# Two-layer encoder on one core: the residual stream kept with features along the partitions, weights stationary in the output projections and in the first MLP's way down

## The chip, the cores and the metric

One core of a Trainium2 chip runs the whole program. The metric is the device time of one launch in microseconds (us). The engines are named as in the profile: PE (matmul, with PEld for its weight loads), DVE (VectorE), ACT (ScalarE), POOL (GpSimd), SP (the DMA queue that loads the weights).

## What is computed

Two residual layers on 256 tokens of 1024 features in float32, each a mixer and an MLP, with RMSNorm before each and at the end:

```python
h = x
for layer in range(2):
    hn = rms_norm(h, norm_mix_g[layer])
    if layer == 0:   # 8 GQA heads and 8 dilated heads, one output projection
        mix = concatenate([o_a, o_b]) @ ab_w_out
    else:            # latent attention, 16 heads: hn @ c_w_down first, then up-projections
        mix = o_c @ c_w_out
    h = h + mix
    hn = rms_norm(h, norm_mlp_g[layer])
    h = h + square(relu(hn @ mlp_w1[layer])) @ mlp_w2[layer]     # 1024 -> 4096 -> 1024
return rms_norm(h, final_norm_g)
```

## The kernel before

Float32 products are made of three matmuls (`mm3`, lines 273 to 278): each operand is split into a high part that the PE reads in its one-pass float32 form and a low remainder, and high x high, high x low and low x high are summed in PSUM. Weights come in chunks of 2048 columns through SP; ACT casts the high half (`whi`, line 223), DVE subtracts for the low half (`wlo`, line 230), and eight buffers of each are held, so that a cast waits for the PE to give back the buffer of an earlier chunk.

A matmul has a stationary operand (128 x 128, loaded by PEld) and a moving one (up to 512 columns). Before the change the residual `xh` lies with tokens along the partitions (two tiles of 128 tokens x 1024 features). The two output projections (`out_first`, `out_second`, lines 545 to 574) and the way down of both MLPs (`down`, line 616) hold 128 tokens stationary and move 512 weight columns. A PSUM bank of 512 columns is one token tile `t` and one half `c` of the features. `residual` (line 508) adds a finished bank to `xh` on DVE. The next projection wants the features along the partitions, as `hT` (high and low, both views of `hTs`), so `turn` (line 516) transposes four 128 x 128 blocks on PE against `ident` (line 521), multiplies by the gain on DVE (line 525), casts on ACT (line 528) and subtracts on DVE (line 529). `Later` puts each turn a quarter of a chunk behind its bank. There are twelve turns: four after each output projection and four after the first MLP. All other projections (`rows` in the way up, lines 601 and 602; the latent down, line 1091; q up, line 1135) already hold the weights stationary.

Division by the root mean square is left to later: `mean_square` (line 350) takes squares of `xh` on ACT with a running sum per token, and the result is used per token in the residual of the MLP (`rs2`) or in `latent` (line 1099), where `rsqrt` on POOL (line 337) and a spread over the partitions (`row_scales`, line 364) follow on the matmuls with `ones` of lines 1102 and 1105. In the meantime PE works on the q up-projection.

In the first attention the order is written out by hand (`ORDER_AB`); elsewhere a scheduler places each engine's instructions by priority, and `tc.high_priority()` moves residual and turn ahead. Each engine runs its list in order. PSUM has four banks `mm`, two `s` and two `o`. `work` is a tile of 512 columns with five buffers.

Of the kernel before, what the change touches and what calls it, by code (L numbers as in the profile page):

```python
# [11 lines left out]
F32 = mybir.dt.float32  # L12
# [157 lines left out]
def encoder(ctx: ExitStack, tc: tile.TileContext, x, xg, wall, grow, const, onehot, relb, out):  # L170
# [116 lines left out]
    g = cp.tile([P, N_G], F32, name="g")  # L287
    xgt = ap.tile([P, N_G + KT * S], F32, name="xgt", tag="OT0")

# [20 lines left out]
    kc = cp.tile([P, N_K], F32, name="kc")  # L310
    xh = cp.tile([P, NT, D], F32, name="xh")
    for i in range(2):
# [29 lines left out]

    def squares(part, t, c):
        nc.scalar.activation(junk, xh[:, t, cols(c, 512)], AF.Square, accum_out=part[:, 2 * c + t:2 * c + t + 1])
# [4 lines left out]

    def mean_square(name):  # L350

        part, u = small(4), cp.tile([P, NT], F32, name=f"u{name}")
        for t in range(NT):
            for c in range(2):
                squares(part, t, c)
        mean_of(part, u)
        return u
# [149 lines left out]

    def residual(acc, t, c, scale=None):
        dst = xh[:, t, cols(c, 512)]
        with tc.high_priority():  # L510
            if scale is None:
                nc.vector.tensor_tensor(dst, acc, dst, op=OP.add)
            else:
                nc.vector.scalar_tensor_tensor(dst, acc, scale, dst, op0=OP.mult, op1=OP.add)

    def turn(c, t, gbase):

        with tc.high_priority():
            pt = t_bank()
            for q in range(4):  # L520
                nc.tensor.transpose(pt[:, cols(q)], xh[:, t, cols(4 * c + q)], ident)  # L521
            ks = slice(4 * c, 4 * c + 4)
            gt = work()
            gv, pv = (z.rearrange("p (k t) -> p k t", k=4) for z in (gt, pt))
            nc.vector.tensor_tensor(gv, pv, g[:, gbase + 4 * c:gbase + 4 * c + 4][:, :, None].to_broadcast([P, 4, P]),
                                    op=OP.mult)
            hi, lo = hT[0][:, ks, cols(t)], hT[1][:, ks, cols(t)]
            nc.scalar.copy(hi, gv)
            nc.vector.tensor_tensor(lo, gv, hi.bitcast(F32), op=OP.subtract)  # L529

    class Later:

        todo = None

        def put(self, *a):
            self.todo = a

        def flush(self):
            if self.todo is not None:
                turn(*self.todo)  # L540
                self.todo = None

    later = Later()
# [12 lines left out]

    def out_second(name, src, acc, gbase):
        last = None
        for c in range(2):
            i, w = take(name, 2 + c, 4)  # L560
            with ExitStack() as order:
                if last is not None:
                    order.enter_context(tc.issue_after(last.ins))
                for t in range(NT):
                    for k in range(4):
                        last = mm3(acc[c][t], tok(src, 4 + k, t), w(k), False, k == 3)
                        if k == 1:
                            quarter()
                            later.flush()
                    if t == 1:  # L570
                        done.add(i)
                    residual(acc[c][t], t, c)
                    later.put(c, t, gbase)
                    quarter()

    def mlp(l, final, store):
        h2, down_w = {}, {}
        acc = {}
        with tc.tile_pool(name=f"mlp{l}", bufs=3) as mp:
# [35 lines left out]

            def down(u, c, t):
                i, w = down_w[u]
                for k in range(2):
                    mm3(acc[c, t], tok(h2[u], k, t), w(k, cols(c, 512)), u + k == 0,
                        k == 1 and u == (14 if final and c == 1 else 15))  # L620

            first = [take(f"w1_{l}", 0, 8)]
            hb = [[s_bank() for _ in range(2)], [mm_bank() for _ in range(2)]]
            for ks in (range(4), range(4, 8)):
                for u in range(2):
                    if len(first) < 2 and u == 1:
                        first.append(take(f"w1_{l}", 1, 8))
                    for m in range(2):
# [5 lines left out]
                        quarter()  # L634
                        later.flush()
            rs2 = cp.tile([P, NT], F32, name=f"rs2{l}")
            nc.vector.reciprocal(rs2, mean_square(f"m{l}"))
            for c in range(2):
                for t in range(NT):
                    acc[c, t] = mm_bank()  # L640
            for u in range(2, 16):
                down_w[u - 2] = take(f"w2_{l}", u - 2, 2)
                for c in range(2):
                    for t in range(NT):
# [3 lines left out]
                        quarter()  # L648
                up(u)
            for u in (14, 15):  # L650
                down_w[u] = take(f"w2_{l}", u, 2)
            groups = [(c, t) for c in range(2) for t in range(NT)]
            if not final:
                for c, t in groups:
                    down(14, c, t)
                    quarter()
                    later.flush()
# [3 lines left out]
                    residual(acc[c, t], t, c, rs2[:, t:t + 1])  # L661
                    later.put(c, t, G_MIX + KT)
                    quarter()
# [390 lines left out]
    with tc.tile_pool(name="l1", bufs=1) as lp:  # L1054
# [29 lines left out]

        u1 = mean_square("c")
        for j in range(2):
            i, w = take("down", j, 4)
            for n, m in enumerate(order):
# [7 lines left out]
                quarter()  # L1096
                later.flush()

# [149 lines left out]
```

## Time and profile before

| | us |
|---|---|
| median of 3 runs (568.02 to 568.09) | 568.04 |
| the profiled execution | 567.76 |
| its span from first to last instruction | 566.0 |
| PE busy in the span | 555.5 |
| PEld / DVE / ACT / POOL busy | 461.6 / 399.1 / 328.5 / 33.5 |

Matmuls overlap in the pipe: one of 512 columns stays on record for 0.39 us while the next starts after 0.23. What a matmul costs a full PE is therefore the distance between starts, which is read from the timeline, and not its duration.

### The profile page before, as it was taken

Reading aid. Unit: us, or ns where it says so; the run is one execution under the profiler, and the core shown is the slowest. Engines: PE = TensorE matmul, PEld = TensorE weight load, DVE = VectorE, ACT = ScalarE, POOL = GpSimd, SP = SyncE. Lnnn points to the kernel's source line nnn. Section 1 sums busy time; section 2 is a strip of 40 time slices with the busy share of each in tenths; the row PEclk is TensorE's granted clock in tenths of the full one; section 3 lists DMA queues with packets and bytes.
Section 4 is the critical chain, followed back from the end, with each engine's and each line's share of the span. In section 5 each row is a group of like instructions: output and inputs, shape, how many; then the busy total and the mean of one; then the engine's idle time right before and its main releaser. Section 6 shows DMA issues by size and latency. Waiting matters only on the chain.

```text
span 566.0 us, 8115 instructions
## 1 busy us (share of the span) xinstructions
PE 555.5 (98%) x3044; PEld 461.6 (82%) x3044; DVE 399.1 (71%) x717; ACT 328.5 (58%) x612; POOL 33.5 (6%) x58
## 2 busy tenths in 40 slices
PE   8999999999999999999999999999999999999994
PEld 4899777888888888888889876678888888888884
DVE  4999978986675666566687987588667566656635
ACT  5879878755444454545464797655544445454513
POOL 3430000000000000000012000000000000000002
PEclk9999999999999999999999999999999999999999
DMA  8847344765555454646426222255555545554101
GB/s 287 356 157 240 125 150 155 259 212 193 174 198 203 170 203 173 218 156 218 167 107 247 75 76 75 75 186 174 198 173 200 201 170 204 172 219 153 71 1 74
DMA packets 16663, 97.16 MB, mean 172 GB/s; under 512 B 1858, under 2 KB 3650, under 8 KB 5872
## 3 DMA queue, kind: packets, MB, share of 16 engines
q1 hardware_dynamic: 15040, 94.38, 46.1%
q0 software_dynamic: 864, 1.20, 1.0%
q10 hardware_dynamic: 720, 1.07, 0.6%
q8 instruction: 24, 0.39, 0.3%
q14 instruction: 15, 0.12, 0.1%
HBM read 95.05 MB, written 1.06 MB: 170 GB/s over the span
## 4 chain that ended last, share of the span: by engine, by line
PE 89%; DMA 3%; ACT 3%; DVE 2%; POOL 1%; issue 1%; SPq 0%; POOLq 0%; DVEq 0%; ACTq 0%
PE s L601 20%; PE mm L276 15%; PE mm L278 15%; PE mm L277 15%; PE s L602 10%; PE s L1205 2%; DMA xh<-in_x 2%; PE o L408 2%; PE o L480 1%; PE o L469 1%; PE o L419 1%; DMA raw<-in_wall 1%; PE o L521 1%; PE mm L601 1%; ACT whi L223 1%
## 5 line engine op out<-in xcount | busy, mean ns | idle before, releaser
L230 DVE TENSOR_TENSOR wlo<-raw,whi 128x1024 fp32r<-128x1024 f32 (+1 forms) x182 | 208.8, 1163 | 96.1 <-ACT whi L223 95.6
L223 ACT CAST whi<-raw 128x1024 fp32r<-128x1024 f32 (+1 forms) x181 | 177.9, 1005 | 83.5 <-PE mm L278 39.1
L601 PE MATMUL s<-hTs,whi 128*128 128x512 f32 x480 | 168.5, 393 | 0.1
L602 PE MATMUL s<-hTs,wlo 128*128 128x256 f32 x480 | 134.3, 280 | 0.0
L601 PEld LDWEIGHTS s<-hTs,whi 128*128 128x128 f32 x480 | 90.2, 188 | 20.4 <-DVE hTs L529 0.4
L276 PE MATMUL mm<-whi,h2h 128*128 128x512 f32 x252 | 99.5, 395 | 0.0
L277 PE MATMUL mm<-wlo,h2h 128*128 128x512 f32 x252 | 99.5, 395 | 0.0
L278 PE MATMUL mm<-whi,h2l 128*128 128x512 f32 x252 | 99.0, 395 | 0.0
L602 PEld LDWEIGHTS s<-hTs,wlo 128*128 128x128 f32 x480 | 90.3, 188 | 1.3
L594 ACT CAST h2h<-work 128x256 fp32r<-128x256 f32 x64 | 25.6, 403 | 56.7 <-DVE work L593 56.7
L276 PEld LDWEIGHTS mm<-whi,h2h 128*128 128x128 f32 x252 | 47.5, 188 | 11.6 <-ACT h2h L594 0.9
L278 PEld LDWEIGHTS mm<-whi,h2l 128*128 128x128 f32 x252 | 47.4, 188 | 11.2 <-DVE h2l L595 0.3
L277 PEld LDWEIGHTS mm<-wlo,h2h 128*128 128x128 f32 x252 | 47.5, 188 | 9.5
L591 ACT COPY work<-s 128x256 f32<-128x256 f32 x60 | 22.2, 371 | 46.4 <-PE s L602 46.4
L592 DVE TENSOR_TENSOR work<-s,work 128x256 f32<-128x256 f32 x60 | 25.2, 420 | 17.1 <-ACT work L591 17.1
L595 DVE TENSOR_TENSOR h2l<-work,h2h 128x256 fp32r<-128x256 f32 x64 | 26.8, 421 | 14.6 <-ACT h2h L594 14.6
L593 DVE SCALAR_TENSOR_TENSOR work<-work 128x256 f32<-128x256 f32 x64 | 27.0, 424 | 2.0
L276 PE MATMUL mm<-whi,hTs 128*128 128x256 f32 (+1 forms) x80 | 27.2, 340 | 0.5 <-ACT hTs L992 0.5
L278 PE MATMUL mm<-whi,hTs 128*128 128x256 f32 (+1 forms) x80 | 26.7, 334 | 0.0
L276 PE MATMUL mm<-whi,OT 128*128 128x512 f32 x64 | 26.5, 414 | 0.0
L277 PE MATMUL mm<-wlo,hTs 128*128 128x256 f32 (+1 forms) x80 | 26.4, 330 | 0.0
L277 PE MATMUL mm<-wlo,OT 128*128 128x512 f32 x64 | 25.7, 401 | 0.0
(236 smaller groups left out, 759.4 us busy)
## 6 DMA issues: line engine op xcount, KB each, us to landing
raw<-in_wall SPq DMA_DIRECT2D x84, 1024.0 KB, 4.8
bias<-line_d SPq DMA_DIRECT2D x4, 384.0 KB, 6.0
raw<-in_wall SPq DMA_DIRECT2D x4, 256.0 KB, 5.8
raw<-in_wall SPq DMA_DIRECT2D x2, 512.0 KB, 7.0
xh<-in_x SPq DMA_DIRECT2D x1, 1024.0 KB, 11.1
xgt<-in_xg SPq DMA_DIRECT2D x2, 256.0 KB, 7.5
kc<-in_const SPq DMA_DIRECT2D x1, 512.0 KB, 8.3
kdB<-kdB POOLq DMA_DIRECT2D x4, 128.0 KB, 4.0
```

Source lines behind the costliest of these rows:

```text
L223: return cast(parts[i, q // 2][0][:, 512 * (q % 2):512 * (q % 2 + n)], raws[i][:, 512 * q:512 * (q + n)])
L230: nc.vector.tensor_tensor(lo[:, s], raws[i][:, 512 * q:512 * (q + n)], hi[:, s].bitcast(F32), op=OP.subtract)
L276: nc.tensor.matmul(out, ah, bh, start=first, stop=False)
L277: nc.tensor.matmul(out, ah, bl, start=False, stop=False)
L278: return nc.tensor.matmul(out, al, bh, start=False, stop=last)
L591: nc.scalar.copy(v[:, 0], bank[:, S:])
L592: nc.vector.tensor_tensor(v[:, 0], bank[:, :S], v[:, 0], op=OP.add)
L593: nc.vector.scalar_tensor_tensor(v[:, 1], v[:, 0], 0.0, v[:, 0], op0=OP.max, op1=OP.mult)
L594: nc.scalar.copy(hi, v[:, 1])
L595: nc.vector.tensor_tensor(lo, v[:, 1], hi.bitcast(F32), op=OP.subtract)
L601: nc.tensor.matmul(bank, wh, hTs[:, k].rearrange("p a t -> p (a t)"), start=k == 0, stop=False)
L602: nc.tensor.matmul(bank[:, S:], wl, hT[0][:, k], start=False, stop=k == 7)
```

## The change

The residual keeps the features along the partitions until the last MLP. The input tile `xgt`, which holds x in this layout, becomes a constant-pool tile and is the residual itself (`xr`); the token-major `xh` moves to the buffer `OT0` and serves the first layer's mean square and, again, the last MLP. The output projections and the first MLP's way down hold weight blocks of 128 x 128 stationary and move all 256 tokens, so each matmul of 512 columns becomes two of 256. `residual` adds a bank and makes `hT` at once from two feature tiles, on ACT (gain and cast) and DVE (gain and subtract); `turn` and `Later` are gone. Squares are summed by `Squares` on ACT and POOL; `spread` gives the mean to all partitions with two matmuls on `ones`, `by_token` gives it per token with four matmuls of one column. The last MLP still wants tokens along the partitions: `xgt` is transposed there, 16 blocks in four banks, and copied by ACT.

```diff
-    xgt = ap.tile([P, N_G + KT * S], F32, name="xgt", tag="OT0")
+    xgt = cp.tile([P, N_G + KT * S], F32, name="xgt")
+    xr = xgt[:, N_G:]
...
-    xh = cp.tile([P, NT, D], F32, name="xh")
+    xh = ap.tile([P, NT, D], F32, name="xh", tag="OT0")
...
+    def residual(bank, b, gbase, scale=None):
+        dst = xr[:, cols(b, 512)]
         with tc.high_priority():
+            if scale is not None:
+                v = work()
+                nc.vector.tensor_tensor(halves(v), halves(bank), scale[:, None, :].to_broadcast([P, 2, S]), op=OP.mult)
+                bank = v
+            nc.vector.tensor_tensor(dst, bank, dst, op=OP.add)
+            for k in (2 * b, 2 * b + 1):
+                gc = g[:, gbase + k:gbase + k + 1]
+                nc.scalar.activation(hT[0][:, k], xT(k), AF.Copy, scale=gc)
+                nc.vector.scalar_tensor_tensor(hT[1][:, k], xT(k), gc, hT[0][:, k].bitcast(F32),
+                                               op0=OP.mult, op1=OP.subtract)
...
+    class Squares:
+        def add(self, b):
+            if b == 0:
+                nc.scalar.activation(self.total, xr[:, cols(b, 512)], AF.Square)
+                return
+            sq = work()
+            nc.scalar.activation(sq, xr[:, cols(b, 512)], AF.Square)
+            nc.gpsimd.tensor_tensor(self.total, self.total, sq, op=OP.add)
+        def by_token(self):
+            pm, u = o_bank(), small(2, 12)
+            for t in range(NT):
+                for i in range(2):
+                    nc.tensor.matmul(pm[:, t:t + 1], self.total[:, S * i + P * t:S * i + P * t + P], ones[:, 0:1],
+                                     start=i == 0, stop=i == 1)
+            nc.vector.tensor_scalar(u, pm[:, :NT], 1.0 / D, EPS, op0=OP.mult, op1=OP.add)
+            return u
+        def spread(self):
+            pm, r = o_bank(), sp.tile([P, S], F32, name="rsb", tag="prob", bufs=3)
+            for i in range(2):
+                nc.tensor.matmul(pm[:, :S], ones, self.total[:, cols(i, S)], start=i == 0, stop=i == 1)
...
     def out_first(name, src, acc):
...
-                for t in range(NT):
-                    mm3(acc[c][t], tok(src, k, t), w(k), k == 0, False)
+                for m in range(4):
+                    mm3(acc[c][m // 2][:, cols(m % 2, S)], w(k, cols(m)), pair(src, ALL, k), k + m % 2 == 0, False)
...
             def down(u, c, t):
                 i, w = down_w[u]
                 for k in range(2):
-                    mm3(acc[c, t], tok(h2[u], k, t), w(k, cols(c, 512)), u + k == 0,
...
+                    else:
+                        for m in range(2):
+                            mm3(acc[c, t][:, cols(m, S)], w(k, cols(4 * c + 2 * t + m)), pair(h2[u], ALL, k),
+                                u + k + m == 0, u + k + m == 17)
...
+            if final:
+                xh = ap.tile([P, NT, D], F32, name="xh", tag="OT0")
+                for t in range(NT):
+                    for c in range(2):
+                        pt = t_bank()
+                        for q in range(4):
+                            nc.tensor.transpose(pt[:, cols(q)], xT(4 * c + q)[:, cols(t)], ident)
+                        nc.scalar.copy(xh[:, t, cols(c, 512)], pt)
...
+                if not final and u == 4:
+                    rsb = sums.spread()
...
-        u1 = mean_square("c")
+        total = Squares()
...
+                if j == 0:
+                    total.add(n)
+        u1 = total.by_token()
```

The scheduler's lists change in three places that matter below. First, DVE behind the first output projection (numbers tell tiles apart), before: `xh_83` is the residual, line 525 the gain of a turn, line 529 its low part.

```order
L512 TENSOR_TENSOR xh_83<-mm_1113,xh_83 128x512
L230 TENSOR_TENSOR wlo_1457<-raw_1250,whi_1456 128x1024
L525 TENSOR_TENSOR work_1355<-o_1350,g_72 128x512
L512 TENSOR_TENSOR xh_83<-mm_1114,xh_83 128x512
L230 TENSOR_TENSOR wlo_1495<-raw_1348,whi_1494 128x1024
L525 TENSOR_TENSOR work_1381<-o_1376,g_72 128x512
L529 TENSOR_TENSOR hTs_99<-work_1355,hTs_99 128x4x128
L512 TENSOR_TENSOR xh_83<-mm_1236,xh_83 128x512
```

and now, with the residual in `xgt_73`:

```order
L517 TENSOR_TENSOR xgt_73<-mm_1113,xgt_73 128x512
L517 TENSOR_TENSOR xgt_73<-mm_1114,xgt_73 128x512
L521 SCALAR_TENSOR_TENSOR hTs_99<-xgt_73,g_72,hTs_99 128x256 x4
L230 TENSOR_TENSOR wlo_1571<-raw_1418,whi_1570 128x1024
L517 TENSOR_TENSOR xgt_73<-mm_1260,xgt_73 128x512
L230 TENSOR_TENSOR wlo_1605<-raw_1418,whi_1604 128x1024
L521 SCALAR_TENSOR_TENSOR hTs_99<-xgt_73,g_72,hTs_99 128x256 x2
L517 TENSOR_TENSOR xgt_73<-mm_1261,xgt_73 128x512
```

A bank's add is followed on DVE by the low parts of its own two feature tiles; the bank of transposes `o`, which line 525 took from PE, is gone.

Second, PE in the latent stage, now (line 365 spreads the scales over the partitions, `cqT` and `whi`/`wlo` are the q up-projection):

```order
L276 MATMUL mm<-cqT_3417,whi 128x256
L365 MATMUL o<-dg,ones 128x128
L277 MATMUL mm<-cqT_3418,whi 128x256
L278 MATMUL mm<-cqT_3417,wlo 128x256
L276 MATMUL mm<-cqT_3417,whi 128x256
L277 MATMUL mm<-cqT_3418,whi 128x256
L278 MATMUL mm<-cqT_3417,wlo 128x256
L365 MATMUL o<-dg,ones 128x128 x3
```

Before, the four stood together as line 364, behind 46 matmuls of the q up-projection counted from line 1102 (16 of them ahead of line 1105). Now the first stands behind 40 (15 of them ahead of line 1133, which is line 1105 of before), and the four matmuls of `by_token` stand ahead of all of these, right behind the latent down.

Third, PE behind the first two ways up of the last MLP, now (line 656 is a transpose of the residual into a bank `o`, two banks in a row; lines 610 and 611 are 601 and 602 of before):

```order
L611 MATMUL mm<-hTs,wlo 128x256
L656 MATMUL o<-kc,xgt 128x128 x8
L276 MATMUL mm<-whi,h2h 128x512
L277 MATMUL mm<-wlo,h2h 128x512
L278 MATMUL mm<-whi,h2l 128x512
L276 MATMUL mm<-whi,h2h 128x512
L277 MATMUL mm<-wlo,h2h 128x512
L276 MATMUL mm<-whi,h2h 128x512
L277 MATMUL mm<-wlo,h2h 128x512
L656 MATMUL o<-kc,xgt 128x128 x8
L278 MATMUL mm<-whi,h2l 128x512 x2
```

Seven matmuls of the way down stand between the two runs of eight transposes. On ACT the two copies that empty the first two banks stand behind the two casts of `h2h` (line 603, line 594 of before), and two more copies behind a square.

## Rows read from the trace of the kernel before

**Rows 1.** The page: busy us (share), instructions; PE's busy tenths in 40 slices.
```profile
PE 555.5 (98%) x3044; PEld 461.6 (82%) x3044; DVE 399.1 (71%) x717; ACT 328.5 (58%) x612; POOL 33.5 (6%) x58
...
PE   8999999999999999999999999999999999999994
```
**Rows 2.** The chain that ended last, by engine.
```profile
PE 89%; DMA 3%; ACT 3%; DVE 2%; POOL 1%; issue 1%; SPq 0%; POOLq 0%; DVEq 0%; ACTq 0%
```
**Rows 3.** Waits: who waited for whom, us in total, times, longest.
```profile
ACT whi L223 <- PE mm L278: 39.1, 31, 1.7
```
**Rows 4.** Timeline of PE, first output projection: first of 15 matmuls, a turn, two matmuls.
```profile
99.64 0.40 PE L278 MATMUL mm<-whi,OT 128*128 128x512 f32 x1
...
103.14 0.60 PE L521 MATMUL o<-kc,xh 128*128 128x128 f32 x4
103.49 0.48 PE L276 MATMUL mm<-whi,OT 128*128 128x512 f32 x1
103.80 0.40 PE L277 MATMUL mm<-wlo,OT 128*128 128x512 f32 x1
```
**Rows 5.** The same, a turn in the second output projection.
```profile
370.30 0.66 PE L521 MATMUL o<-kc,xh 128*128 128x128 f32 x4
370.71 0.48 PE L277 MATMUL mm<-wlo,OT 128*128 128x512 f32 x1
```
**Rows 6.** Timeline of PE, a way up of the last MLP.
```profile
385.17 0.28 PE L602 MATMUL mm<-hTs,wlo 128*128 128x256 f32 x1
385.56 0.50 PE L601 MATMUL s<-hTs,whi 128*128 128x512 f32 x1
```
**Rows 7.** Timeline of PE, a way down: first of 24 matmuls, and what follows them.
```profile
402.34 0.39 PE L276 MATMUL mm<-whi,h2h 128*128 128x512 f32 x1
...
407.92 0.40 PE L601 MATMUL s<-hTs,whi 128*128 128x512 f32 x1
```
**Rows 8.** Timeline of PE, latent down: first of 72 matmuls, what follows, next stream.
```profile
294.29 0.28 PE L276 MATMUL mm<-hTs,whi 128*128 128x256 f32 x1
...
302.83 0.50 PE L1102 MATMUL o<-ones,ckg 128*128 128x1 f32 x4
303.20 0.37 PE L276 MATMUL mm<-cqT,whi 128*128 128x256 f32 x1
```
**Rows 9.** Timeline of PE, first attention: first of 24 matmuls, and what follows them.
```profile
40.40 0.28 PE L276 MATMUL mm<-whi,hTs 128*128 128x256 f32 x1
...
43.28 0.28 PE L938 MATMUL s<-kdA,qA 128*128 128x256 f32 x1
```
**Rows 10.** Groups by line and form: busy us, mean ns, idle before: weights' low halves, loads.
```profile
L230 DVE TENSOR_TENSOR wlo<-raw,whi 128x1024 fp32r<-128x1024 f32 x162 | 195.2, 1220 | 92.4 <-ACT whi L223 92.0
...
L276 PEld LDWEIGHTS mm<-whi,h2h 128*128 128x128 f32 x252 | 47.5, 188 | 11.6 <-ACT h2h L594 0.9
```
**Rows 11.** Timeline of PE and ACT, end of the last MLP's first two ways up.
```profile
391.21 0.39 PE L276 MATMUL mm<-whi,h2h 128*128 128x512 f32 x1
...
392.51 0.71 ACT L594 CAST h2h<-work 128x256 fp32r<-128x256 f32 x2
```
**Rows 12.** Timeline of PE and ACT: full float32 matmuls of 256 columns; copies out of PSUM.
```profile
317.68 1.89 PE L1205 MATMUL s<-kT,qT 128*128 128x256 f32 x8
319.22 0.47 PE L276 MATMUL mm<-ckT,whi 128*128 128x256 f32 x1
...
316.15 2.32 ACT L1171 COPY vC<-mm 128x512 f32<-128x512 f32 x4
```
**Rows 13.** Timeline of PE, latent stage, with the idle time and its releaser.
```profile
305.18 0.50 PE L1105 MATMUL o<-ones,sqs 128*128 128x1 f32 x4
...
309.07 0.28 PE L276 MATMUL mm<-cqT,whi 128*128 128x256 f32 x1
309.98 1.13 PE L364 MATMUL o<-dg,ones 128*128 128x128 f32 x8 [0.64 <-DVE dg L363]
310.87 0.36 PE L277 MATMUL mm<-cqT,whi 128*128 128x256 f32 x1
```

More of the change, by code (lines that the diff above doesn't have):

```diff
@@ L341, in rsqrt, with squares @@
         nc.gpsimd.tensor_tensor(dst, y, z, op=OP.mult)
-    def squares(part, t, c):
+    def squares(part, t, c, xh=xh):
         nc.scalar.activation(junk, xh[:, t, cols(c, 512)], AF.Square, accum_out=part[:, 2 * c + t:2 * c + t + 1])
@@ L354, in mean_square @@
             for c in range(2):
-                squares(part, t, c)
+                squares(part, t, c, xh)
         mean_of(part, u)
@@ L506, in scaled_softmax @@
         return {"max": mx, "exp": ex, "flip": False}
-    def residual(acc, t, c, scale=None):
-        dst = xh[:, t, cols(c, 512)]
+    def residual(bank, b, gbase, scale=None):
+        dst = xr[:, cols(b, 512)]
         with tc.high_priority():
[L511 to L543, printed above, removed]
+            if scale is not None:
[3 more added lines that the diff above has]
+            nc.vector.tensor_tensor(dst, bank, dst, op=OP.add)
@@ new lines, in residual, with __init__ @@
+            for k in (2 * b, 2 * b + 1):
[4 more added lines that the diff above has]
+    class Squares:
+        def __init__(self):
+            self.total = work()
+        def add(self, b):
[17 more added lines that the diff above has]
+                nc.tensor.matmul(pm[:, :S], ones, self.total[:, cols(i, S)], start=i == 0, stop=i == 1)
+            nc.vector.tensor_scalar(r, pm[:, :S], 1.0 / D, EPS, op0=OP.mult, op1=OP.add)
+            nc.vector.reciprocal(r, r)
+            return r
@@ L563, in out_second @@
                     order.enter_context(tc.issue_after(last.ins))
-                for t in range(NT):
+                for m in range(4):
                     for k in range(4):
[L566 to L570, printed above, removed]
+                        last = mm3(acc[c][m // 2][:, cols(m % 2, S)], w(k, cols(m)), pair(src, ALL, 4 + k), False, k + m % 2 == 4)
+                    if m == 3:
                         done.add(i)
-                    residual(acc[c][t], t, c)
-                    later.put(c, t, gbase)
+                    if m % 2:
+                        residual(acc[c][m // 2], 2 * c + m // 2, gbase)
                     quarter()
@@ L618, in down @@
                 for k in range(2):
-                    mm3(acc[c, t], tok(h2[u], k, t), w(k, cols(c, 512)), u + k == 0,
-                        k == 1 and u == (14 if final and c == 1 else 15))
+                    if final:
+                        mm3(acc[c, t], tok(h2[u], k, t), w(k, cols(c, 512)), u + k == 0,
+                            k == 1 and u == (14 if c == 1 else 15))
+                    else:
+                        for m in range(2):
+                            mm3(acc[c, t][:, cols(m, S)], w(k, cols(4 * c + 2 * t + m)), pair(h2[u], ALL, k),
+                                u + k + m == 0, u + k + m == 17)
             first = [take(f"w1_{l}", 0, 8)]
@@ L634, in mlp @@
                         quarter()
-                        later.flush()
-            rs2 = cp.tile([P, NT], F32, name=f"rs2{l}")
-            nc.vector.reciprocal(rs2, mean_square(f"m{l}"))
+            if final:
+                xh = ap.tile([P, NT, D], F32, name="xh", tag="OT0")
[5 more added lines that the diff above has]
+                        nc.scalar.copy(xh[:, t, cols(c, 512)], pt)
+                rs2 = cp.tile([P, NT], F32, name="rs2")
+                nc.vector.reciprocal(rs2, mean_square("m", xh))
+            else:
+                sums = Squares()
+                for b in range(4):
+                    sums.add(b)
             for c in range(2):
@@ L656, in mlp @@
                     quarter()
-                    later.flush()
                     down(15, c, t)
@@ L660, in mlp @@
                         done.update(down_w[u][0] for u in (14, 15))
-                    residual(acc[c, t], t, c, rs2[:, t:t + 1])
-                    later.put(c, t, G_MIX + KT)
+                    residual(acc[c, t], 2 * c + t, G_MIX + KT, rsb)
                     quarter()
@@ L1096, in encoder @@
                 quarter()
-                later.flush()
+                if j == 0:
+                    total.add(n)
+        u1 = total.by_token()
         def latent():
```

2 lines of the change are left out of this document (1 added, 1 removed).

## The prediction

> **What bounds the kernel now.** The page comes first: PE is busy in 98% of the span and in nine tenths of every slice but the first and the last [rows 1], so the time is PE's list, added up, plus the places where it stands still. The chain of waits agrees: 89% of the chain that ended last lies on PE [rows 2]. Third, the waits: ACT's casts of weights wait for PE to give buffers back [rows 3]. Weights are therefore prepared as far ahead as the buffers go, and work that moves between ACT and DVE has cover; if that cover were gone, each late cast would show as idle time of PE ahead of lines 276 to 278. So I cost the change on PE's list, from the distance between starts in its timeline, and then look for the places where the new list must wait.
>
> **What goes: twelve turns.** A turn in the first output projection takes PE from 103.14 to 103.49, 0.35 us, and the matmul behind it holds the engine 0.31 us instead of 0.23 [rows 4]: 0.35 + 0.08. Another takes 0.41 us, with the same 0.08 behind it [rows 5]. Eight of the twelve are of the first kind (0.35 or 0.36, in the mean 0.44 with what follows) and four of the second: 8 x 0.44 + 4 x 0.49 = 5.5, **-5.5 us**. With the turns goes the one place in the last layer where PE waited for a turn's end on DVE: 385.17 to 385.56 is 0.39 us where a matmul of 256 columns takes 0.12 [rows 6], **-0.3 us**. What is late there next is the weights, and they have cover [rows 3].
>
> **What is cut in two.** In the first MLP's way down 16 chunks x 4 groups x 2 x 3 = 384 matmuls of 512 columns become 768 of 256; in the two output projections 2 x 2 x 4 x 2 x 3 x 2 = 192 become 384. The columns stay the same. A way down moves 24 matmuls from 402.34 to 407.92, 232.5 ns each [rows 7]; the output projection 15 in 3.50 us, 233.3 ns [rows 4]. The latent down already has the new form, weights stationary and 256 tokens moving: 72 matmuls from 294.29 to 302.83, 118.6 ns each, with ACT and DVE at work beside it [rows 8]. A cut therefore costs 2 x 118.6 - 232.5 = 4.7 ns in the way down and 3.9 ns in the projections: 384 x 4.7 + 192 x 3.9 = **+2.55 us**. The shorter run in the first attention is dearer, 24 in 2.88 us, 120.0 ns [rows 9]; it has tokens stationary, so I take the first value. Bounds: nothing, if halves cost half; +4.15 at 120.0 ns (1152 x 1.4 ns = 1.6 more).
>
> The Trainium skill ("TensorE: Matmul & The Clock Gate", Back-to-back issue gap) gives columns over 2.4 GHz plus about 2.5 ns from one start to the next. By it 256 columns take 109.2 ns, 512 take 215.8, and a cut costs 2.5 ns, so 1.4 us would stand in place of 2.55 and the time would come to 568.0. No row agrees: both forms lie 9 to 17 ns above it [rows 7, 8], and the rows decide.
>
> **What PE gets in addition.** Sixteen transposes in the last MLP, in two runs of eight. A transpose starts every 0.11 us and a run ends with the same 0.08: 8 x 0.11 + 0.08 less the short step behind the last one, 0.87 a run, 1.75 together. The second run needs two banks that ACT must empty. PE ends the ways up at 391.21 by the old clock; ACT is busy with two casts of `h2h` until 393.22 [rows 11], then copies two banks at 0.58 us each [rows 12] until 393.8 and 394.4. PE gets there at 391.21 + 0.87 + 7 x 0.2325 = 393.7. The first four transposes wait 0.1, the next about as much: **+1.95 us** with the wait. Between 1.75, if the copies come first, and 3.0, if a cast of 1 us slips ahead of them.
>
> `spread`: two full float32 matmuls of 256 columns. Four take 1.54 us [rows 12], two 0.77, plus 0.08: **+0.85 us**. Its total is made two ways up earlier, so nothing waits.
>
> `by_token` and the latent stage. A full float32 matmul is two records, here 0.11 us apart: eight take 309.98 to 310.87 [rows 13], and of two matmuls of one column the four take 0.37 [rows 8]. Four more matmuls are eight records, 0.9 us. They stand ahead of the chain that PE already waits for: line 1105 at 305.18, scales on POOL, line 364 at 309.98, 4.80 us, with PE idle behind its last matmul from 309.07 + 0.12 on, 0.8 us [rows 13]. The chain is as long after the change, but PE has five matmuls less of the q up-projection between its ends (25 instead of 30), 0.6 us, and waits that much longer. The four spread matmuls stand apart, one more change of stream, 0.08: 0.9 + 0.6 + 0.08, **+1.55 us**. Between 1.0, if the chain shortens so that the longer wait doesn't come, and 2.2, if the three later scales, behind an evacuation of 0.6 us on DVE, hold PE once more. POOL's part of `by_token`, two small operations, runs beside the 15 matmuls ahead of line 1133.
>
> Off PE: ACT makes the high part of each feature tile and DVE the low part, where gain, cast and subtract stood; ACT squares later than before, POOL makes six adds. The weights' lead covers this [rows 3]. At the end of the first MLP DVE mixes up to three low halves of weights, 1.2 us each [rows 10], with scale, add and two tiles of the last bank: by my count 5.6 us to the last tile, which PE needs 57 matmuls behind the bank, at 6.8 us. So it costs nothing.
>
> **The sum** against the profiled execution: -5.5 - 0.3 + 2.55 + 1.95 + 0.85 + 1.55 = +1.1 us. That execution took 567.76 us, 1.8 more than its span of 566.0; the median of the runs is 568.04, 0.28 above it. From the median I forecast **569.1 us**. A measurement of this kernel tells about 0.2% from no change, which is 1.14 us: the forecast lies just inside that border, on the slow side.
>
> **The rivals.**
> 1. Slower: cut matmuls at 120.0 ns. Long runs with a weight load for every 118 ns, beside ACT and DVE at their full load, could settle at the dearer row. For it: rows 9; against it: 72 in a row at 118.6 [rows 8]. Price 1152 x 1.4 ns = 1.6 us more: 570.7. A tenth of a nanosecond over 118.6 already carries the sum past 1.14.
> 2. Slower: PE waits for `hT` between the first MLP and the latent down. My count leaves 1.2 us there. Two low halves of weights more ahead of the last bank, 2.4 us [rows 10], would use it up and cost 1.2 us: 570.3. For it: the bank needs a scale of its own now. Against it: PE has never waited there, and the list shows three such halves, not five.
> 3. Faster: halves cost half, so the 2.55 us fall away: 566.6. For it: the columns are as many as before. Against it: no run of 256 columns in the trace lies at 116 ns [rows 8, 9].
> 4. Weight loads that are not hidden. A load stays on record for 188 ns [rows 10]; if it did not overlap the running matmul, no start could follow the last in under 188 ns, and 1152 x (188 - 118.6) ns = 80 us would come on top: 649. The Trainium skill says so for loads into the rows in use ("TensorE: Matmul & The Clock Gate", Part 3: Packing small matmuls: a load overlaps only where the row group differs). By that rule the change would be a heavy loss. The trace disagrees: starts follow at 118.6 ns with a load each [rows 8].
>
> That the change doesn't do what it says would show as transposes left over; 16 are, and they are in the sum.
>
> **How the numbers follow.** The forecast's case gets 0.68; with its terms a little to either side it spans 568.0 to 570.2, and since it lies at the border, 0.39 of it is within 0.2%, 0.28 slower and 0.01 faster. Rival 1 gets 0.13 and rival 2 0.05, both slower. Rival 3 gets 0.13, 0.09 of it faster and 0.04 within, if only a part of the 2.55 us falls away. Rival 4 gets 0.01 at most. Together: faster 0.10, within 0.43, slower 0.47. The range runs from 567.0, which leaves the full rival 3 out, to 571.0, which takes in rivals 1 and 2; of the bounds above, both ends of the cut, the chain's and the transposes' lie in it one at a time.
>
> **What would show it.** No line 521 on PE; way-down runs of 48 matmuls at 118.6 ns (5.69 us where 5.58 stood); the idle time ahead of line 365 near 1.2 us where the profile counted 0.64; two runs of eight transposes with under 0.5 us of idle time before the second. Idle time of PE ahead of lines 276 to 278 behind the first MLP would prove rival 2; starts at 120 ns in the way down rival 1. A time under 567.0 or over 571.0 would mean that a term is missing from the sum.

## The result, and the profile after

| | us |
|---|---|
| kernel before, median of 4 runs (567.95 to 568.09) | 568.03 |
| changed kernel, median of 4 runs (573.60 to 574.05) | 573.93 |
| ratio, 95% interval | 1.0102 (1.0089 to 1.0114) |
| span of the profiled execution, before and after | 566.0 and 571.8 |

The change costs 5.9 us (5.1 to 6.5 by the interval), where 1.1 was forecast. The time lies 2.9 us above the range, and by the prediction's own last sentence a term is missing. The runs found two; about 1 us stays open.

The page of the changed kernel, PE's line and the chain by engine, answers to [rows 1, 2]:

```profile
PE 558.0 (98%) x3600; PEld 490.7 (86%) x3600; DVE 402.8 (70%) x723; ACT 332.3 (58%) x620; POOL 39.0 (7%) x60
...
PE 83%; DVE 6%; ACT 4%; DMA 3%; issue 2%; POOL 1%; SPq 0%; POOLq 0%; DVEq 0%; ACTq 0%
```

PE is as full as it was, but the chain that ended last has six points less on PE: somewhere PE now waits for DVE. First the terms of the sum, in the timeline of PE (start, duration, line and operation, count, idle time ahead): a way down of the first MLP, `by_token`, `row_scales`, and the transposes of the last MLP.

```profile
268.63 0.28 PE L276 MATMUL mm<-h2h,whi 128*128 128x256 f32 x1
...
274.30 0.39 PE L610 MATMUL s<-hTs,whi 128*128 128x512 f32 x1
...
304.84 0.95 PE L543 MATMUL o<-ones,work 128*128 128x1 f32 x8
305.64 0.58 PE L1130 MATMUL o<-ones,ckg 128*128 128x1 f32 x4
...
312.75 0.46 PE L365 MATMUL o<-dg,ones 128*128 128x128 f32 x2 [1.24 <-DVE dg L364]
...
393.59 1.03 PE L656 MATMUL o<-kc,xgt 128*128 128x128 f32 x8
394.38 0.48 PE L276 MATMUL mm<-whi,h2h 128*128 128x512 f32 x1
...
396.43 1.03 PE L656 MATMUL o<-kc,xgt 128*128 128x128 f32 x8
397.22 0.48 PE L278 MATMUL mm<-whi,h2l 128*128 128x512 f32 x1
```

They came out as worked out: the way down takes 5.67 us (forecast 5.69; before 5.58, [rows 7]), `by_token` 0.80 (0.9), the wait ahead of line 365 is 1.24 us (0.64 + 0.6; [rows 13]), a run of transposes 0.79 and 0.08 for the matmul behind it (0.87). Most of the missing time must therefore lie where the sum has no term. The starts of the same operations in both timelines give the place, counted from the span's start:

| point on PE | before | after | difference |
|---|---|---|---|
| first matmul of the first output projection | 78.31 | 77.89 | -0.42 |
| latent down, start | 291.00 | 291.57 | +0.57 |
| latent down, end | 302.83 | 305.64 | +2.81 |
| first scores of the latent attention | 317.68 | 321.01 | +3.33 |
| last values of the latent attention | 365.43 | 369.64 | +4.21 |
| last MLP, first matmul of its way down | 391.21 | 394.38 | +3.17 |
| end of PE | 558.22 | 564.07 | +5.85 |

**First place: the latent down** loses 2.24 us: `by_token` adds 0.8, a wait with what follows it 1.76, slower matmuls (119.9 ns from start to start instead of 118.7) 0.1, and a turn that stood in this stretch takes 0.44 off. The timelines of PE, DVE and POOL there:

```profile
299.78 0.39 PE L277 MATMUL s<-hTs,whi 128*128 128x256 f32 x1 [1.46 <-DVE hTs L521]
...
294.55 1.53 DVE L521 SCALAR_TENSOR_TENSOR hTs<-xgt,g,hTs 128x256 fp32r<-128x256 f32 x1
296.00 2.32 DVE L230 TENSOR_TENSOR wlo<-raw,whi 128x1024 fp32r<-128x1024 f32 x1
298.24 1.88 DVE L521 SCALAR_TENSOR_TENSOR hTs<-xgt,g,hTs 128x256 fp32r<-128x256 f32 x2
...
294.45 4.99 POOL L536 TENSOR_TENSOR work<-work 128x512 f32<-128x512 f32 x3 [165.78 <-ACT work L535]
```

PE stands still for 1.46 us, waiting for a low tile of `hTs`: the wait of the second rival. From start to start it is 1.74 us where 0.12 is usual, and the next matmuls lose 0.14 more. But DVE has no work more than was counted. While POOL makes its three adds, a tile's low part takes 1.53 us instead of 0.48, and a weight's low half 2.32 instead of 1.22 [rows 10].

**Second place: the last MLP** loses 2.7 us behind the first run of transposes. The second run with the waits around it is 1.2 of them (394.38 to 397.22 less seven matmuls of 0.2325), for which the sum had 1.1; the other 1.5 come in its 14 full steps (periods) of 24 matmuls down and 32 up, which are the same in both kernels. The first matmul of two steps that follow each other, in the timeline of PE, before:

```profile
535.94 0.39 PE L276 MATMUL mm<-whi,h2h 128*128 128x512 f32 x1
...
547.07 0.39 PE L276 MATMUL mm<-whi,h2h 128*128 128x512 f32 x1
```

and after:

```profile
541.70 0.39 PE L276 MATMUL mm<-whi,h2h 128*128 128x512 f32 x1
...
552.94 0.39 PE L276 MATMUL mm<-whi,h2h 128*128 128x512 f32 x1
```

A step takes 11.24 us instead of 11.13, in every step alike, with no idle time on record. From a matmul of 512 columns in the ways up to the next start there are 235.9 ns instead of 229.9 (mean of 240). What differs is where the tiles lie, by the addresses in the built programs: with `xgt` in the constant pool and `xh` in `OT0`, the weights (first buffer of `whi`) begin at byte 55392 of a partition instead of 55328, `hTs` at 129120 instead of 129216, `h2h` at 179520 instead of 179616.

### The profile page after: what moved, and what is told of

It is laid out like the page before. It is cut to its first block, busy times and chain, and to the rows that moved or that the text cites. A ratio compares the mean times of both kernels' runs of the same rounds, so it can differ in the third digit from the quotient of the medians.

```text
span 571.8 us, 9259 instructions
## 1 busy us (share of the span) xinstructions
PE 558.0 (98%) x3600; PEld 490.7 (86%) x3600; DVE 402.8 (70%) x723; ACT 332.3 (58%) x620; POOL 39.0 (7%) x60
## 4 chain that ended last, share of the span: by engine, by line
PE 83%; DVE 6%; ACT 4%; DMA 3%; issue 2%; POOL 1%; SPq 0%; POOLq 0%; DVEq 0%; ACTq 0%
PE s L610 19%; PE mm L276 14%; PE mm L278 14%; PE mm L277 14%; PE s L611 10%; DMA xh<-in_x 2%; PE s L1233 2%; PE o L409 2%; DVE wlo L230 1%; PE o L420 1%; ACT whi L223 1%; PE mm L610 1%; PE o L470 1%; PE o L481 1%; DMA raw<-in_wall 1%
## 5 line engine op out<-in xcount | busy, mean ns | idle before, releaser
L276 PE MATMUL mm<-h2h,whi 128*128 128x256 f32 x256 | 71.9, 282 | 0.1
L277 PE MATMUL mm<-h2l,whi 128*128 128x256 f32 x256 | 71.7, 281 | 0.0
L278 PE MATMUL mm<-h2h,wlo 128*128 128x256 f32 x256 | 71.7, 281 | 0.0
L276 PE MATMUL mm<-whi,h2h 128*128 128x512 f32 x124 | 49.1, 396 | 0.1
L276 PEld LDWEIGHTS mm<-h2h,whi 128*128 128x128 f32 x256 | 48.0, 188 | 1.1 <-ACT h2h L603 0.5
L277 PE MATMUL mm<-wlo,h2h 128*128 128x512 f32 x124 | 49.0, 395 | 0.0
L278 PE MATMUL mm<-whi,h2l 128*128 128x512 f32 x124 | 48.9, 396 | 0.0
L277 PEld LDWEIGHTS mm<-h2l,whi 128*128 128x128 f32 x256 | 48.2, 188 | 0.0
L278 PEld LDWEIGHTS mm<-h2h,wlo 128*128 128x128 f32 x256 | 48.2, 188 | 0.0
L276 PE MATMUL mm<-OT,whi 128*128 128x256 f32 x128 | 37.1, 291 | 0.0
L277 PE MATMUL mm<-OT,whi 128*128 128x256 f32 x128 | 36.1, 283 | 0.0
```

Source lines behind the costliest of these rows:

```text
L276: nc.tensor.matmul(out, ah, bh, start=first, stop=False)
L277: nc.tensor.matmul(out, ah, bl, start=False, stop=False)
L278: return nc.tensor.matmul(out, al, bh, start=False, stop=last)
```

## The experiments

The kernel before, timed beside each group, took 567.80 us for the first four kernels, 568.13 for the next four (a_both, a_n3, b_cut, b_sh96) and 568.09 for the three named h2.

### The tiles' places alone: a_res and b_res

```diff
-    xh = ap.tile([P, NT, D], F32, name="xh", tag="OT0")
+    xh = ap.tile([P, NT * D + 36], F32, name="xh", tag="OT0")[:, :NT * D].rearrange("p (t d) -> p t d", t=NT)
```

> The changed kernel with one tile made wider: the token-major `xh` gets 36 columns more in the buffer OT0, so that `hTs`, `work`, `pts`, `h2h` and `h2l` lie, modulo 64 bytes, where they lay in the kernel before (hTs 0, h2h 32 instead of 32 and 0). No instruction changes its place in any list. What it asks: in the last MLP, whose 56 matmuls per chunk pair are the same in both kernels, a period took 11.13 us before and 11.24 us after. Theory P (placement of the tiles in SBUF): the period falls back to 11.13 us and the time by about 1.5 us, or by 2 with the first MLP's ways up: 571.9 to 572.6. Theory Q (other work beside it, or the longer list of PE): period 11.24, time 573.9 within 0.3.

Measured: 572.23 us (ratio to before 1.0075, 1.0062 to 1.0088). The same two points as above:

```profile
540.41 0.39 PE L276 MATMUL mm<-whi,h2h 128*128 128x512 f32 x1
...
551.54 0.39 PE L276 MATMUL mm<-whi,h2h 128*128 128x512 f32 x1
```

The period is back at 11.13 us. And the other way round, in the kernel before:

```diff
-    xgt = ap.tile([P, N_G + KT * S], F32, name="xgt", tag="OT0")
+    xgt = ap.tile([P, N_G + KT * S + 8], F32, name="xgt", tag="OT0")
```

> The kernel before with one tile made wider: `xgt` gets 8 columns more, so that `hTs`, `work`, `pts`, `h2h` and `h2l` lie, modulo 64 bytes, where they lie in the changed kernel. The lists are those of the kernel before. Theory P (placement): the period of the last MLP rises from 11.13 to about 11.24 us and the time from 568.0 to 569.5 to 570.2. Theory Q (other work, or the longer list): period 11.13, time 568.0 within 0.3.

Measured: 570.24 us (1.0043, 1.0030 to 1.0057), 2.4 us slower for 32 bytes that nobody reads.

```profile
538.25 0.39 PE L276 MATMUL mm<-whi,h2h 128*128 128x512 f32 x1
...
549.49 0.39 PE L276 MATMUL mm<-whi,h2h 128*128 128x512 f32 x1
```

The period is 11.24, in both MLPs. Theory P holds on both kernels, with each kernel's list of instructions unchanged; Q falls. From here on the *distance* of two operands is the address at which the stationary tile begins less that of the moving one, modulo 256 bytes. In the ways up it is 96 in the kernel before and in a_res, 0 in the changed kernel and 64 in b_res.

### Every tile at a multiple of 64: a_al64

```diff
+    pad0 = cp.tile([P, 8], F32, name="pad0")
...
+        pad1 = sp.tile([P, 8], F32, name="pad1", tag="pad1", bufs=1)
```

> The changed kernel with two unused tiles of 8 columns, one behind `ones` and one behind `sums`, so that the weights `whi` and `wlo`, `hTs`, `work`, `pts`, `h2h` and `h2l` all begin at a multiple of 64 bytes (in the changed kernel the weights and `hTs` lie 32 beyond one). Theory P (placement): the ways up with `hTs` at 0 and the ways down with the weights at 0 both speed up: a period of 11.1 us or less in the last MLP, and a time under 572.6. Theory Q: 573.9 within 0.3.

Measured: 573.89 us (1.0108, 1.0095 to 1.0122). The period of the last MLP is 11.11, but the time is no better: theory P as put here (under 572.6) misses. The ways down of the last MLP sped up (about 228 ns a matmul, 233 in the changed kernel), the ways up did not (235.8), and the first MLP's way down became dearer (119.9 ns, 118.3), which took a period there from 11.23 to 11.36 us in the mean. So alignment as such is not the rule. By the addresses the ways up have the same distance, 0, here as in the changed kernel, and the kernel before and a_res share 96: in the last MLP equal distance goes with equal time.

### The adds on DVE: a_dve

```diff
-            nc.gpsimd.tensor_tensor(self.total, self.total, sq, op=OP.add)
+            nc.vector.tensor_tensor(self.total, self.total, sq, op=OP.add)
```

> The changed kernel with the running sum of `Squares.add` on DVE instead of POOL (one word, six adds of 128x512). What it asks: in the latent down PE waits 1.46 us for the last low tile of `hTs`, while three DVE operations beside POOL's adds take 1526, 2318 and 1486 ns where such operations otherwise take 480, 1220 and 480. Theory S (POOL's adds slow DVE down): those three fall back to 0.5, 1.2 and 0.5 us, the wait of 1.46 us goes or shrinks to under 0.5, and the time falls by 1.0 to 1.7 us, to 572.2 to 572.9; the adds on DVE, about 0.6 us each, are mostly behind the tiles that PE waits for. Theory T (DVE is simply late: its list holds a weight's low half between scale and tiles): DVE has more work now, the wait grows, and the time is 573.9 or above, up to 575.

Measured: 572.53 us (1.0081, 1.0067 to 1.0094). DVE's timeline in the same place:

```profile
295.33 0.48 DVE L521 SCALAR_TENSOR_TENSOR hTs<-xgt,g,hTs 128x256 fp32r<-128x256 f32 x1
295.73 0.68 DVE L536 TENSOR_TENSOR work<-work 128x512 f32<-128x512 f32 x1
296.33 0.87 DVE L521 SCALAR_TENSOR_TENSOR hTs<-xgt,g,hTs 128x256 fp32r<-128x256 f32 x2
297.12 0.68 DVE L536 TENSOR_TENSOR work<-work 128x512 f32<-128x512 f32 x1
297.73 1.22 DVE L230 TENSOR_TENSOR wlo<-raw,whi 128x1024 fp32r<-128x1024 f32 x1
```

DVE has three adds of 0.68 us more in this stretch and is done earlier; PE's wait of 1.46 us is gone. PE, ACT and SP have the same lists as in the changed kernel. Theory S holds: POOL's adds stretched DVE's operations.

### Both together: a_both

> The changed kernel with both edits: the wider `xh` that brings the tiles back to the places of the kernel before (modulo 64 bytes), and the adds of `Squares` on DVE. Alone they gave 1.7 us (573.9 to 572.2) and 1.4 us (573.9 to 572.5). If the two causes are separate, they add up: 570.8 within 0.4, 3.0 us above the kernel before, of which my sum accounts for 1.1. If both act through the same thing (DVE operations that hold the matmuls up), less than the sum is left: 571.5 or above.

Measured: 570.28 us (1.0039, 1.0026 to 1.0053), 2.15 above the kernel before, where the changed kernel lies 5.9 above: 3.75 gone. Against the kernel before in their calls, the edits alone gave 1.5 and 1.2, with intervals of 0.7 either way; the profiles are sharper. The first matmul of the first output projection comes at 77.89 to 78.67 us in these executions, so I count from there to the end: after 493.94 us, a_res 491.89, a_dve 492.18, a_both 490.07. That is 2.05 and 1.76 alone and 3.87 together: they add up. (The times alone had led me to expect 570.4 at the least; 570.28 is just under it.)

Part of what is left above the forecast, 2.15 against 1.1, may be two waits that the kernel before does not have, in the two attentions:

```profile
97.86 0.65 PE L481 MATMUL o<-pts,vB 128*64 128x256 f32 x4 [0.31 <-ACT pts L475]
...
324.32 0.48 PE L1233 MATMUL s<-kT,qT 128*128 128x256 f32 x1 [0.64 <-ACT prob L504]
```

Ahead of the second, the timeline of DVE has a low half of weights between the maximum (line 499) and its scaling (line 500), for which the exponential on ACT waits:

```profile
321.14 0.68 DVE L499 TENSOR_REDUCE sm<-s 128x2 f32<-128x512 f32 x1
321.74 1.21 DVE L230 TENSOR_TENSOR wlo<-raw,whi 128x1024 fp32r<-128x1024 f32 x1
322.87 0.15 DVE L500 TENSOR_TENSOR sm<-sm,both 128x2 f32<-128x2 f32 x1
```

That is a reading of the timeline; no run took these waits away. They are not the only ones: at the end of the first MLP a matmul of a_both starts 0.36 us after the last where 0.12 is usual (283.92).

### The wait in the latent stage: a_n3

```diff
-            if n == 2:
+            if n == 3:
                 with tc.issue_after(last.ins):
```

> The kernel of the run above (both edits) with the second half of `latent` placed behind the fourth group of q up-projections, not the third: 33 matmuls instead of 25 stand between line 1133 and the first matmul of `row_scales` on PE. My step said that PE waits there longer because five matmuls fewer stand between the ends of the same chain. If so, 8 x 0.118 = 0.95 us of the idle time ahead of line 365 (1.2 us) go and the time falls by about 0.9 against the run above. If the chain itself were held up by PE's own order (POOL or DVE start later), the idle time stays above 1 us and the time is the same.

Measured: 570.27 us (1.0040, 1.0028 to 1.0053), the same as a_both.

```profile
311.21 0.46 PE L365 MATMUL o<-dg,ones 128*128 128x128 f32 x2 [0.29 <-DVE dg L364]
311.91 0.60 PE L365 MATMUL o<-dg,ones 128*128 128x128 f32 x3 [0.24 <-DVE dg L364]
...
319.67 0.70 PE L1233 MATMUL s<-kT,qT 128*128 128x256 f32 x2 [0.40 <-DVE kT L1187]
```

Both theories miss. The idle time ahead of line 365 fell from 1.24 to 0.29 us, as my step said, but 0.24 and 0.40 came back behind it, and the first scores come at 319.67 instead of 319.31. As I read it, the chain over POOL, DVE and ACT sets the time through this stage, and work that PE does earlier only moves PE's waits. So the 0.6 us of the sum were the size of the wait, but taking the wait away gave no time back: that the five matmuls were its price is not shown.

### The cut alone: b_cut

```diff
-                    mm3(acc[c][t], tok(src, k, t), w(k), k == 0, False)
+                    for m in range(2):
+                        mm3(acc[c][t][:, cols(m, S)], tok(src, k, t), w(k, cols(m, S)), k + m == 0, False)
```

and the same in `out_second` and the first MLP's `down`.

> The kernel before with only the cut: in the two output projections and the first MLP's way down each matmul of 512 columns is made as two of 256, the 128 tokens stay stationary and the weights stay the moving operand; turns and the residual are as before. My term: 576 matmuls become 1152, +2.55 us, 570.4 (118.6 ns each). If the start distance depends on where the operands lie, as the moved tiles suggest, 256 columns can be dearer or cheaper in this form: 120 ns gives 572.0, 116.3 ns (half of 232.5) gives 567.8.

Measured: 571.30 us (1.0059, 1.0046 to 1.0071): +3.2 (2.6 to 4.0) against the forecast 2.55. A period of the first MLP goes from 11.13 to 11.25 us, 0.12 x 16 = 1.9, where the term had 1.8. The cut's price was right within 0.7 us here, where the operands are not exchanged: the cut costs this much without the exchange.

### Place or distance: b_sh96

```diff
+    pad = cp.tile([P, 24], F32, name="pad")
```

> The kernel before with one unused tile of 24 columns (96 bytes) ahead of the weights' buffers: everything from `raw` on lies 96 bytes further, so the weights and `h2h`, `h2l` begin at a multiple of 128 bytes, and all of these tiles lie to each other as before. In the run with the tiles at multiples of 64 the ways down of the last MLP, with both operands at a multiple of 128, went at 228 ns a matmul instead of 232.5. If it is the absolute place that counts there, each of the 15 chunks of a way down gains 24 x 4.5 ns = 0.11 us in both MLPs, about 3 us together: 564.8, faster than both kernels. If only the distance of the two operands from each other counts, nothing changes: 567.8.

Measured: 567.90 us (0.9997, 0.9988 to 1.0006), periods of 11.13. Everything from `raw` on moved by 96 bytes and nothing changed: it is not the absolute place that counts.

### Distance on an idle chip: micro

```diff
+        for n, t in zip(NM, sta):
+            bank = ps.tile([P, 512], F32, name="wide" + n, tag="bank", bufs=4)
+            for i in range(36):
+                nc.tensor.matmul(bank, t[:, P * (i % 4):P * (i % 4) + P], mov[:, i // 2 % 4], start=i == 0, stop=i == 35)
```

> A kernel of its own that computes nothing of the reference and writes zeros: 16 stationary tiles of 2080 bytes each lie one behind the other, so that with A at 0 modulo 512 bytes from the moving tile each next one lies 32 bytes further (A, B, ... P). For each, 36 matmuls of 512 columns and then 36 of 256, with DVE, ACT and the DMA queues idle. Theory D (the start distance depends on the distance of the two operands' addresses): the groups differ by several ns, repeatably, and the pairs that occur in the encoder stand out as there: for 512 columns I (256) fastest, near 228, A and K near 235; for 256 columns K (320) near 113.5, A near 120. Theory D2 (the address matters only through conflicts with DVE's, ACT's or DMA's accesses): with the other engines idle all groups are alike, within 1 ns.

Measured, timeline of PE, a row for each group of 36:

```profile
24.94 8.33 PE L39 MATMUL wideA<-mov,stA 128*128 128x512 f32 x36
33.11 8.55 PE L39 MATMUL wideB<-mov,stB 128*128 128x512 f32 x36
...
83.33 8.56 PE L39 MATMUL wideH<-mov,stH 128*128 128x512 f32 x36
91.72 8.33 PE L39 MATMUL wideI<-mov,stI 128*128 128x512 f32 x36
99.89 8.55 PE L39 MATMUL wideJ<-mov,stJ 128*128 128x512 f32 x36
...
158.50 4.47 PE L43 MATMUL halfA<-mov,stA 128*128 128x256 f32 x36
162.81 4.42 PE L43 MATMUL halfB<-mov,stB 128*128 128x256 f32 x36
...
171.31 4.39 PE L43 MATMUL halfD<-mov,stD 128*128 128x256 f32 x36
175.53 4.43 PE L43 MATMUL halfE<-mov,stE 128*128 128x256 f32 x36
```

The tiles A to P lie at distances 0, 32, 64 and so on. The time between the starts of two groups, divided by 36 (good to 0.3 ns, as starts are given to 0.01 us): A 226.9 ns, H 233.1, I 226.9. The pattern repeats after eight tiles, 256 bytes: 512 columns take 226.9 ns at distance 0, 229.2 at 192 (G) and 232.5 to 233.9 at the others. For 256 columns it is the other way about: 119.7 ns at 0 and 117.2 at 96 (D). D2 falls: no other engine is at work. The ways down of the last MLP fit: `h2h` lies 128 from the weights in the kernel before, 232.4 ns there and 232.5 here (E), and 224 in the changed kernel, 233.3 there and 233.1 here (H). But A and K were misjudged: I had read their value from the ways up, where matmuls of 512 and 256 columns alternate. The latent down's 113.5 ns at K, from b_res, did not come back either (117.8). Nor is the latent down the same wherever its distance is 96: 118.7 ns in the kernel before, b_sh96 and b_h2m, 117.3 in a_both, a_n3 and a_h2m, and 117.2 here (D). So the distance is not all that counts.

### The same place for `h2` in the kernel before: b_h2m and b_h2p

```diff
         with tc.tile_pool(name=f"mlp{l}", bufs=3) as mp:
+            pad = mp.tile([P, 992], F32, name="pad", bufs=1)
```

> The kernel before with an unused tile of 3968 bytes ahead of `h2h` and `h2l` in both MLPs, which brings them, modulo 512 bytes, 256 from the weights instead of 384; nothing else moves. That is the distance at which the last MLP's way down went at 228 ns a matmul in the run with all tiles at multiples of 64. Theory D (distance of the operands): 24 x 4.6 ns less in each chunk, periods of 11.02 us instead of 11.13 in both MLPs, 31 chunks, 3.4 us less: 564.5 to 565.2, faster than both kernels. If the absolute place counted: unchanged, 568.0.

Measured: 564.15 us (0.9932, 0.9920 to 0.9945), faster than both kernels.

```profile
532.71 0.39 PE L276 MATMUL mm<-whi,h2h 128*128 128x512 f32 x1
...
543.71 0.39 PE L276 MATMUL mm<-whi,h2h 128*128 128x512 f32 x1
```

11.00 us a period. With 32 columns in place of 992:

> The same with an unused tile of 128 bytes: `h2h` and `h2l` at 0 modulo 512 bytes from the weights. By theory D with a pattern that repeats every 256 bytes: as the run above, 565. With a pattern of 512 bytes the ways up show 235.9 ns at distance 0, so the ways down would be dearer, 24 x 3 ns a chunk, 2 us more: 570.

Measured: 564.32 us (0.9934, 0.9922 to 0.9947): the pattern of 256 bytes, as on the idle chip.

### The same in the changed kernel: a_h2m

```diff
+                pad = mp.tile([P, 992], F32, name="pad", bufs=1)
```

on top of a_both, in the last MLP alone.

> The changed kernel with the wider `xh`, the adds on DVE, and in the last MLP alone `h2h` and `h2l` 3968 bytes further, 256 modulo 512 from the weights. Theory D: periods of the last MLP 11.02 us instead of 11.14, 1.8 us less than the run with both edits: 568.5, level with the kernel before within 0.2%. Without an effect: 570.3.

Measured: 568.51 us (1.0007, 0.9998 to 1.0016), level with the kernel before, as expected.

### The ways up on an idle chip: micro2

```diff
+                nc.tensor.matmul(bank, hi, mov[:, i % 4], start=i == 0, stop=False)
+                nc.tensor.matmul(bank[:, S:], lo, mov[:, i % 4, :S], start=False, stop=i == 23)
```

> A second kernel of its own that computes nothing of the reference and writes zeros: the pattern of the ways up, a matmul of 512 columns and one of 256 in turn, each with a stationary block of its own, 24 such pairs for each of eight stationary tiles A to H that lie 0, 32, ... 224 bytes modulo 256 from the moving tile; the other engines are idle. In the encoder a pair took 347.4 ns at the distance of the kernel before (96, D), 352.7 in the changed kernel (0, A) and 352.8 at 64 (C). Theory D (distance alone): D comes out near 347 and A and C near 353 here too, although 512 columns alone were fastest at A (226.7). Theory D2 (in the ways up it is the other engines' traffic that makes A and C dear): all near 347, or A the fastest as in the first kernel of its own.

Measured, timeline of PE, the first matmul of each group of 24 pairs:

```profile
20.94 0.39 PE L40 MATMUL pairA<-mov,stA 128*128 128x512 f32 x1
...
29.41 0.39 PE L40 MATMUL pairB<-mov,stB 128*128 128x512 f32 x1
...
37.90 0.40 PE L40 MATMUL pairC<-mov,stC 128*128 128x512 f32 x1
...
46.36 0.40 PE L40 MATMUL pairD<-mov,stD 128*128 128x512 f32 x1
...
54.69 0.40 PE L40 MATMUL pairE<-mov,stE 128*128 128x512 f32 x1
```

A pair takes 352.9 ns at A, 353.8 at B, 352.5 at C and 347.1 at D, as in the last MLP (352.7 at A, 352.8 at C, 347.4 at D). The kernel before had the ways up at D, the cheapest of these, and the change moved them to A; no other engine is needed to make A dear.

But at A the distance does not settle it alone. Two ways up of the changed kernel, both at distance 0, the first in the first MLP, the second in the last; from the first line of each to the second there are 12 pairs:

```profile
207.66 0.39 PE L610 MATMUL s<-hTs,whi 128*128 128x512 f32 x1
...
211.82 0.39 PE L610 MATMUL s<-hTs,whi 128*128 128x512 f32 x1
...
435.58 0.40 PE L610 MATMUL s<-hTs,whi 128*128 128x512 f32 x1
...
439.82 0.40 PE L610 MATMUL s<-hTs,whi 128*128 128x512 f32 x1
```

That is 347 ns a pair and 353. In the changed kernel most ways up of the first MLP run at the lower value and all but one of the last MLP at the higher; in a_al64, also at 0, those of the first MLP mostly take turns, one at 347, the next at 354. At 96 every one that nothing interrupts runs at 347, at 64 (b_res) at 353. What picks the value at 0 is open; the ways down between them are in halves in the first MLP and whole in the last.

## Why the prediction was wrong

Right in size were the terms that can be read one by one. The cut of a way down, `by_token`, the longer wait ahead of line 365 and the runs of transposes came within 0.1 us of their working; `spread` took 0.68 us from its first record to the next stream and 0.19 more on the matmul behind it, 0.87 where 0.85 stood. For the wait ahead of line 365 that may be luck: a_n3 took most of it away and won nothing. Rival 3 did not happen. Rival 1 did not happen where it was priced, in the long runs of the way down (118.2 ns); the output projections, a third of the cut matmuls, did go at 119.6, 0.4 us in all, and in a_both, with the tiles moved back, at 118.6. With both missing causes taken out (a_both), the sum of 1.1 stands beside 2.15 measured. The two new waits for ACT, 0.31 and 0.64, are about as large as the rest; that they are its cause was only read, not tried, and the rest stays open.

Two steps failed.

**"ACT squares later than before, POOL makes six adds. The weights' lead covers this."** I priced POOL's adds by POOL's own idle time and not by what they do to DVE. Three adds cost DVE 1.05 + 1.10 + 1.0 = 3.2 us (1.53, 2.32 and 1.88 us for what takes 0.48, 1.22 and 0.87), in the one place where PE waits for fresh low tiles. With the adds on DVE the wait was gone and the time fell by 1.2 us (1.76 by the profiles). The stretch used up the 1.2 us of slack of rival 2 without the "two low halves more" that I had made its condition; its price, 1.2 us, was near the wait of 1.46 seen. The Trainium skill says it ("SBUF — State Buffer", SBUF: two separate sides): DVE and GpSimd share a pair of ports as an exclusive lock, also against DVE operations with two inputs in SBUF. The trace agrees, with 1.53 us beside a POOL add and 0.48 without. The rule changes a term of the sum, and I did not use it.

**The buffers' move had no term.** "The input tile becomes a constant-pool tile" was read as a change of names. It moved every later tile, and 1.5 to 2 us (a_res, by the times and by the profiles) went to the distances, most of it in matmuls that the change does not touch. I took 118.6 and 232.5 ns for properties of the form; they belong to the form at the distance at which its operands happened to lie, and at some distances to the stretch as well (347 or 353 ns a pair at distance 0).

The fourth rival stayed as unlikely as it was: starts at 118 ns with a load each.

## What to carry to other kernels

Where a change moves or resizes a buffer ahead of PE's operands, compare the distance of stationary and moving tile modulo 256 bytes before and after, and the starts of a stretch that did not change: here 32 unused bytes cost 2.4 us, and 128 or 3968 gave 3.8 and 3.9. Before a change of form is judged by its time, try both kernels with a pad; at the best places found, the token-major kernel stays ahead, 564.15 against 568.51 us, though the changed one was moved in its last MLP only. Work that goes to POOL "because it is idle" is priced on DVE, at the place where DVE's results are awaited.

## What the runs showed of the hardware

- The time between starts of matmuls depends on the distance of the two operands' addresses modulo 256 bytes, with no other engine at work: 226.9 to 233.9 ns for 512 columns (cheapest at 0), 117.2 to 119.7 for 256 (cheapest at 96, dearest at 0 and 160), 347.1 to 353.8 for a pair of both among the distances shown. A common shift of 96 bytes changes nothing (567.90 us). In the encoder the distance is not the whole rule: at 0 a way up ran at 347 or at 353 ns a pair, and the latent down took 118.7 or 117.3 ns at 96, and 113.4 at 64, where the idle chip has 117.8. The Trainium skill ("TensorE: Matmul & The Clock Gate", Step-by-step: what each phase is for) has two independent read ports, so that a weight load takes nothing from the running matmul. No run took the loads away, so whether they are what the distance acts through stays open; that the distance counts is shown.
- An add of two 128x512 tiles on POOL beside DVE's operations of two SBUF inputs: 4.99 us for three, and the DVE operations beside it last 1.0 to 1.1 us longer each. On DVE the same add takes 0.68.
